# Stores queued behind their data, row tables read 128 columns wide, and the first maxima in another order, in a hybrid Fourier and attention layer

## The chip, the core and the metric

The kernel runs on one core of a Trainium2 chip. The metric is the device time of one execution in microseconds (us), here the median of three runs. The engines have short names in the profile: PE is TensorE (matmuls), PEld its weight loads, DVE is VectorE, ACT is ScalarE, POOL is GpSimd, and SP is SyncE, whose queue issues most of the DMAs. A "q" behind a name (SPq) is that engine's instruction queue.

## The reference

One layer (DEPTH is 1) over 16 meta tokens and 4096 tokens, 4112 rows of 1024 columns. What is computed, cut to its core:

```python
h = concat([meta, x])                                   # 4112 x 1024
u = rmsnorm(h, norm_g)
f_in, f_gate, q, k, v, a_gate = split(u @ w_in)         # 512, 512, 512, 128, 128, 512 columns
fr = real(fftn(f_in as (4112, 8 groups, 64), axes=(rows, 64)))
f_out = (einsum(fr, w_fmix) + b_fmix) * silu(f_gate)
q, k = rope(rmsnorm(q)), rope(rmsnorm(k))               # 8 query heads, 2 key/value heads of 64
a_out = softmax(q k^T / 8) v * silu(a_gate)
h = h + concat([f_out, a_out]) @ w_out
out = rmsnorm(h, final_g)[16:]
```

All tensors are float32. The kernel splits each operand into a float16 high and low part and multiplies three times (high by high, high by low, low by high).

## The kernel before

**Phase A** (`phase_a`, the first 720 us of the profile) goes over 33 row tiles `t` (32 of 128 rows and one of the 16 meta rows). For each tile, `xload` loads the transposed rows, `xsplit` makes the two halves `xh` (ACT, L318) and `xl` (POOL, L319), and `proj` multiplies by the weights: 256 columns of k and v in `tile_kv`, 512 of q in `tile_q`, and twice 512 of gates in `tile_gate`. `xsplit` of the next tile stands ahead of `tile_kv` of the present one, so the halves are made a tile ahead. `tile_kv` also makes the two halves of v (`vst`, ACT L366 and POOL L367, in three buffers `vsb`) and stores them to DRAM (L368, by the helper `store`, L222). `tile_norm` and `tile_stack` finish q and k, and `tile_tr`, which is called a tile later, stores k (by the same helper) and q (on ACT's queue).

Beside the tiles runs the first half of the Fourier group. Each fold `i` (0 to 8) loads 128 columns of rows at four mirrored places (`fold_load`: row scales `rb`, L452, and data `sg`, L454), scales them on POOL (`fold_scale`, L463), adds and subtracts them on DVE (`fold_add`), splits them (`fold_hi`, `fold_lo`) and multiplies them by the Fourier weights of the columns (`fproj`). `fproj` with k = 1 writes results: its inner `put` makes two halves `ahl` (ACT L522, POOL L523, two buffers) and stores them to `acs_d` (L524). Folds 0 to 3 call `put` once and store a part `ge_d` (L532); folds 4 to 7 load that part again (`even_load`, L486) and call `put` three times. The rows of `w_out` are split beside this too (`wo_load`, `wo_split`, stored at L600).

The order of this work is written by hand: `plan` maps slots, four to a tile, to lists of calls, and `deal(slot)` emits them. Fold `i` begins at slot 8 + 23i/2; `w_out` begins at slot `WO0` = 72.

All loads and stores that go through `dma` (`nc.sync.dma_start`) stand in SP's queue in the order in which they are emitted. SP issues them one after another, and waits at a store until its data is there.

**Phase B** (`phase_b`, from 720 us on) is the attention: 32 pairs, one for each of 8 query blocks and 4 head pairs, each with 66 units (`stream`, `step`: two heads by 33 key tiles). A unit multiplies k by q (L1185 to L1194), takes the exponential on ACT (L1199), a rest `rr` on POOL or DVE (L1201), and multiplies by v (L1216 to L1223). For the next pair, 16 groups of row maxima run along (`max_units`: four matmuls L1106, ACT L1111 and DVE L1112 twice each, with four PSUM banks `m`); `red` reduces them to `nm` (DVE L1139), `fin` turns `nm` with a matmul (L1146) and `put` writes the rows into `qB` (ACT L1152, DVE L1153, with a constant `diag`), which the pair's first matmul with `qB` reads (L1190).

Ahead of the first pair stands a prelude: 16 groups and a meta unit for pair 0, and two groups (`AHEAD`) for pair 1, without any attention between.

The second half of the Fourier group (the transform over rows) is a list `flist` that `f_step` takes entries from: "d" is one matmul of a row set with its table (`dft_units`, L895 and L898), "gather" takes the result out of PSUM, "t" is a turn (`trans`, L937 to L944) or the mixing with `w_fmix` and gate (`mix`: matmuls by `mm3`, L86 to L88; early, in the prelude, ACT L990 and POOL L996 and L998; later DVE L992 and POOL L1000), and "gap" lets a unit pass. The first and the last row set (`LAST`) have only 4 rows; their tables `cl` hold 4 columns for each matmul. In the prelude each group is followed by `f_step(11, 2, True)`; then each of the first 264 units calls `f_step(2, 1)` in `block0` until the list is empty. `mix` puts its stores to `mf_d` on a list `held`, which `release` issues (L924) at the next "gather"; its buffers `mos` hold two row sets. When the list is empty, `block0` loads the weights `woh` and `wol` (L1090, L1091), and an assert wants that before unit 258. From pair 4 on, 28 of the pairs carry the output projection of a block (`out_units`, L1296).

Of the kernel before, what the change touches and what calls it, by code (L numbers as in the profile page):

```python
# [32 lines left out]
P = 128  # L33
# [21 lines left out]
def emit(tc, a):  # L55
# [4 lines left out]
    with top:  # L60
# [49 lines left out]
        cl = sh1.tile([P, 2, 2, 18, 4], F16, tag="cl", name="cl")  # L110
# [39 lines left out]
def phase_a(tc, a, pool, mm3, id16, id32, sc):  # L150
# [25 lines left out]
    with ExitStack() as st:  # L176
# [174 lines left out]
        def tile_kv(t):  # L351

            n = xs[t][0]
            rt = rw[:n, pos[t]:pos[t] + 1]
            if t < NT:
                z = live[t] = {k: w2.tile([P, 10, HD], F32, tag=k, name=k) for k in ("sq", "t1", "t2")}
            else:
                z = live[t] = {k: wp.tile([P, 2, HD], F32, name=k + "m") for k in ("sq", "t1", "t2")}
            o = z["o"] = 0 if t < NT else 8
            kvp = proj(t, 0, 256)  # L360
            kp = kvp[:, :P].rearrange("p (h c)->p h c", c=HD)
            S.activation(z["sq"][:n, 8 - o:10 - o], kp, AF.Square, scale=rt)
            vs = w2.tile([P, 2, HD], F32, tag="vs", name="vs")
            S.activation(vs[:n], kvp[:, P:].rearrange("p (h c)->p h c", c=HD), AF.Copy, scale=rt)
            vst = vsb[pos[t] % 3]
            S.activation(vst[:n, :, 0:64], vs[:n], AF.Copy)  # L366
            G.tensor_tensor(out=vst[:n, :, 65:129], in0=vs[:n], in1=vst[:n, :, 0:64], op=ALU.subtract)  # L367
            store(v_d[place[t], :n], vst[:n])  # L368
            rot(t, kp, 8, 10, 1)
# [54 lines left out]
        def tile_tr(t):  # L424
            n, ks = xs.pop(t)[0], kst(t)
            z = live.pop(t)
            store(k_d[place[t] * P:place[t] * P + n], ks[:n].rearrange("p a w b c->p (a w b c)"))
            if t < NT:
                adma(q_d[t * P:(t + 1) * P], z["qs"].rearrange("p h a c->p (h a c)"))
# [53 lines left out]

        def even_load(i):
            fst["ge", i] = w1.tile([P, 512], F32, tag="ge", name="ge")
            dma(fst["ge", i], ge_d[7 - i])  # L486

        def fproj(i, k, x):

# [27 lines left out]
            else:  # L517
                f = fst.pop(("f", i, x))

                def put(g, ty, j):  # L520
                    hl = w2.tile([P, 2, NC_], F16, tag="ahl", name="ahl")[:, :, :nn]
                    S.activation(hl[:, 0], g, AF.Copy)  # L522
                    G.tensor_tensor(out=hl[:, 1], in0=g, in1=hl[:, 0], op=ALU.subtract)  # L523
                    dma(acs_d[ty, :, j, :, cs], hl)  # L524
# [6 lines left out]
                if i < 4:  # L531
                    dma(ge_d[i, :, cs], g)  # L532
                else:

                    ge = fst["ge", i][:, cs]
                    h = w1.tile([P, NC_], F32, tag="fe1", name="fe1")[:, :nn]
                    V.tensor_tensor(out=h, in0=ge, in1=g, op=ALU.add)
                    put(h, 0, 7 - i + 4 * x)
                    V.tensor_tensor(out=g, in0=ge, in1=g, op=ALU.subtract)
                    put(g, 0, 7 - i + 4 * (1 - x))  # L540

        def tail():

# [51 lines left out]
        def wo_split(d):  # L595
            wt, hl = room[:, d % 2], room[:, 2 + d % 2].bitcast(F16).rearrange("p (w c) -> p w c", w=2)
            S.activation(hl[:, 0], wt, AF.Copy, scale=WS)
            V.scalar_tensor_tensor(out=hl[:, 1], in0=wt, scalar=WS, in1=hl[:, 0], op0=ALU.mult, op1=ALU.subtract)
            for w in range(2):
                dma(wo_d[w, :, d], hl[:, w])  # L600


        FOLD0, PER2, SLOTS, WO0 = 8, 23, 4, 72
# [43 lines left out]
        for d in range(10):  # L647
            if d > 1:
                at(WO0 + 3 * d, wo_split, d - 2)
            if d < 8:  # L650
# [133 lines left out]
def phase_b(tc, a, pool, mm3, id32, id16, sc):  # L784
# [10 lines left out]
    with ExitStack() as st:  # L795
# [18 lines left out]
        for t in qB[1]:  # L814
            G.memset(t[0:64], 0.0)
# [3 lines left out]
        V.tensor_copy(diag, id32[0:8, 0:8].unsqueeze(2).broadcast_to([8, 8, P]))  # L819
# [30 lines left out]
        def fix_load():  # L850
            dma(bias, a["bias"])
            V.memset(stk8[0:64], 0.0)
# [19 lines left out]
        def dft_units(i, part, spare):  # L872

            u, odd = seq[i], int(i < 5)
            if part == 0:
                fcur["ct"] = ld["cl"][:, 1 - odd] if u is LAST else ld["cts"].pop(0)
            ct, src = fcur["ct"], ld["acs"][odd]
            mms = []
# [10 lines left out]
            def one(x, slot, chunk, w, first, last):  # L889
# [3 lines left out]
                r = ps[0][0:4 if u is LAST else P, cs]  # L893
                if chunk == 8:
                    T.matmul(r, ct[0:96, x, slot], src[0:96, 8, 0, cs], start=False, stop=last,  # L895
                             skip_group_check=True)
                else:
                    T.matmul(r, ct[:, x, slot + (w == 2)], src[:, chunk, int(w == 1), cs],  # L898
# [23 lines left out]
        def release():  # L922
            while held:
                dma(*held.pop(0))  # L924
# [53 lines left out]
        def mix(u, k, early):  # L978
# [16 lines left out]
            if early:  # L995
                G.tensor_tensor(out=mo[:n], in0=mo[:n], in1=bias[:n].unsqueeze(1).broadcast_to([n, 2, 512]),  # L996
                                op=ALU.add)
                G.tensor_tensor(out=mo[:n], in0=mo[:n], in1=fgu[:n], op=ALU.mult)  # L998
            else:
                G.tensor_tensor(out=mo[:n, ver], in0=mo[:n, ver], in1=fgu[:n, ver], op=ALU.mult)  # L1000
            for ver in vers:
                for p0, w, t0, st in runs_of(u, ver):
                    held.append((rows(mf_d, t0, w, st), mo[p0:p0 + w, ver]))
# [6 lines left out]
        fcur = {}  # L1010

        def f_fill():
            done = []
            for i, u in enumerate(seq):
# [4 lines left out]
                for k, n in enumerate(parts):  # L1019
# [3 lines left out]
                    if i > 4:  # L1023
                        flist.append(("gap", 3))
# [14 lines left out]
        GAPS = (4, 3, 2)  # L1039
        f_fill()  # L1040

        def f_step(n, heavy, early=False):

            while flist:
# [17 lines left out]
                elif k == "gather":  # L1062
# [4 lines left out]
                    release()  # L1067
# [300 lines left out]
        while gs:  # L1368
# [6 lines left out]
            if n == 1:  # L1375
                ld["k_load"](ld["rest"])
            elif n in (7, 10, 13, 16):
# [15 lines left out]
        for k in range(AHEAD):  # L1393
# [4 lines left out]
            if k:  # L1398
                f_step(5, 1, True)
                fin()  # L1400
                put()
                f_step(INIT - 5, 1, True)
# [4 lines left out]
        def block0(g, mid):  # L1407
# [4 lines left out]
            if g < 4 * 66:  # L1412
                f_step(2, 1)
# [185 lines left out]
def shape_constants():  # L1599
# [84 lines left out]
    return {"dch": dch.astype(f), "cd": cd, "cl": cl, "rope": rope, "sgn": sgn}  # L1684
# [54 lines left out]
```

## Time and profile before

| what | value |
|---|---|
| three runs | 3126.31, 3130.44, 3131.52 us; median 3130.44 us |
| the profiled execution | 3128.15 us, its span 3126.4 us, so 1.75 us lie outside the span |
| busy over the span | PE 98%, DVE 72%, ACT 65%, PEld 57%, POOL 55% |
| granted TensorE clock | 0.995 on the mean |
| PE in the chain that ended last | 70% of the span |
| DMA | 235.16 MB, 75 GB/s on the mean |

The profile is of one execution. A row of the timeline has the start in us from the span's start, the time it took in us, the engine, the line, the operation, the tiles as out<-in, the shape and the count, and, in brackets, the idle time of the engine just before it with what ended it. A row of the waits names who waited for whom, with the total in us, the number of times and the longest. A row of the windows has the stretch, its length, then for each engine the busy us and the number of instructions, and at the end the granted TensorE clock, the busy share of the DMA engines and their GB/s. Matmul times are modelled with their latency, so the distance from one start to the next tells what a matmul costs in a dense stream.

### The profile page before, as it was taken

The page shows a single profiled execution, that of the slowest core. Times are in us where ns is not written, and L with a number is a line of the kernel's source. Part 1 is how long each engine was busy: PE and PEld are TensorE (multiplying, and loading weights), DVE is VectorE, ACT ScalarE, POOL GpSimd, SP SyncE. Part 2 cuts the span into 40 slices and gives each one's busy share as a digit, 9 for nine tenths or more (in the row PEclk, how much of TensorE's full clock was granted, in tenths as well). Part 3 has the DMA queues.
Part 4 walks back from the last instruction along what each step waited for, and adds up shares of the span by engine and source line. Part 5 has one row for each costly group of instructions (what it writes and reads, how often), then busy time and mean ns, then how long its engine had stood idle before and what let it go on. Part 6 is the DMA issues. An engine that isn't in the chain of part 4 may idle for free.

```text
span 3126.4 us, 80138 instructions
## 1 busy us (share of the span) xinstructions
PE 3055.6 (98%) x32000; PEld 1792.2 (57%) x32000; DVE 2261.6 (72%) x4866; ACT 2017.9 (65%) x3936; POOL 1732.5 (55%) x1629
## 2 busy tenths in 40 slices
PE   8999999898899999999999999999999999999998
PEld 4555555455566555555555555555555555555564
DVE  7655655565878777777777777777777777777775
ACT  6334233234777677777777777777777777777763
POOL 4665555543666555555555555555555555555553
PEclk9999999999999999999999999999999999999999
DMA  7445444466531221112111211211121112111112
GB/s 254 159 148 180 143 137 141 130 174 201 144 87 32 83 44 37 35 29 49 39 29 29 49 39 29 52 32 29 39 49 29 29 35 52 32 32 29 33 45 71
DMA packets 236763, 235.16 MB, mean 75 GB/s; under 512 B 136948, under 2 KB 180948, under 8 KB 233572
## 3 DMA queue, kind: packets, MB, share of 16 engines
q1 hardware_dynamic: 222564, 204.87, 22.8%
q10 hardware_dynamic: 13824, 25.17, 2.1%
q8 instruction: 250, 4.10, 0.5%
q14 instruction: 125, 1.02, 0.1%
HBM read 131.08 MB, written 66.38 MB: 63 GB/s over the span
## 4 chain that ended last, share of the span: by engine, by line
PE 70%; POOL 4%; DVE 3%; issue 3%; ACT 3%; DMA 2%; SPq 1%; ACTq 0%; POOLq 0%; DVEq 0%
PE o L1216 12%; PE po L1296 9%; PE o L1223 8%; PE s L1189 8%; PE s L1190 7%; PE s L1185 7%; PE m L1106 7%; PE s L1194 5%; PE o L1221 2%; PE o L1219 2%; PE m L1538 1%; ACT pe L1199 1%; POOL rr L1201 1%; PE pd L898 1%; DMA acs_d<-ahl 1%
## 5 line engine op out<-in xcount | busy, mean ns | idle before, releaser
L1199 ACT ACTIVATE pe<-s 128x512 f32<-128x512 f32 x2112 | 1240.1, 610 | 587.9 <-PE s L1194 524.5
L1201 POOL TENSOR_TENSOR rr<-pe 128x512 f16<-128x512 f32 x1014 | 1131.5, 1132 | 824.5 <-ACT pe L1199 819.2
L1201 DVE TENSOR_TENSOR rr<-pe 128x512 f16<-128x512 f32 x1098 | 886.4, 811 | 274.6 <-ACT pe L1199 271.4
L1223 PE MATMUL o<-VV,rr 128*128 128x65 f16 x8448 | 974.8, 193 | 0.3 <-POOL rr L1201 0.3
L1223 PEld LDWEIGHTS <-rr 128*128 128x128 f16 x8448 | 784.5, 98 | 188.1 <-issue 1.4
L1112 DVE CUSTOM_DVE_ANT_0 rl<-m,rl 128x512 f32<-128x512 f32 x1024 | 703.5, 689 | 242.1 <-ACT rl L1111 240.8
L1216 PE MATMUL o<-VV,pe 128*128 128x129 f16 x6336 | 839.5, 221 | 0.8 <-ACT tt L1230 0.8
L1216 PEld LDWEIGHTS <-pe 128*128 128x128 bf16 x6336 | 589.7, 97 | 364.7 <-issue 192.6
L1111 ACT ACTIVATE rl<-m 128x512 f32<-128x512 f32 x1024 | 630.2, 617 | 9.9 <-PE m L1106 5.8
L1190 PE MATMUL s<-qB,K 128*128 128x512 f16 x1088 | 412.0, 379 | 3.5 <-DVE qB L1153 3.5
L1189 PE MATMUL s<-qA,K 128*128 128x512 f16 x1088 | 411.2, 378 | 2.5 <-ACT pe L1199 1.7
L1219 PE MATMUL o<-VV,pe 128*128 128x65 f16 x2112 | 411.3, 195 | 0.0
L1221 PE MATMUL o<-VV,pe 128*128 128x64 f16 x2112 | 410.5, 194 | 0.0
L1185 PE MATMUL s<-qA,K 128*128 128x512 f16 x1024 | 387.5, 378 | 7.9 <-ACT pe L1199 6.5
L330 PE MATMUL ps<-wh,xh 128*128 128x512 f16 (+2 forms) x1032 | 354.2, 355 | 13.1 <-ACT xh L318 12.9
L331 PE MATMUL ps<-wl,xh 128*128 128x512 f16 (+2 forms) x1032 | 354.0, 354 | 2.2 <-DVE wl L301 2.2
L1106 PE MATMUL m<-K,qA 64*128 64x512 f16 x1024 | 305.1, 377 | 9.5 <-ACT rl L1111 6.6
L1106 PE MATMUL m<-K,qB 64*128 64x512 f16 x1024 | 310.9, 377 | 2.1 <-DVE mx L1112 1.6
L333 PE MATMUL ps<-wh,xl 128*128 128x512 f16 x768 | 291.4, 379 | 0.0
L1221 PEld LDWEIGHTS <-pe 128*128 128x128 bf16 x2112 | 209.1, 99 | 0.0
L1219 PEld LDWEIGHTS <-pe 128*128 128x128 bf16 x2112 | 206.5, 98 | 0.0
L1194 PE MATMUL s<-qB,K 64*128 64x512 f16 x512 | 197.9, 387 | 0.0
(219 smaller groups left out, 4368.9 us busy)
## 6 DMA issues: line engine op xcount, KB each, us to landing
room<-x SPq DMA_DIRECT2D x32, 512.0 KB
xt<-xt SPq DMA_DIRECT2D x32, 512.0 KB
sg<-fx SPq DMA_DIRECT2D x16, 1024.0 KB
xr<-x SPq DMA_DIRECT2D x32, 512.0 KB
out<-yo SPq DMA_DIRECT2D x32, 512.0 KB
fg_d<-g ACTq DMA_DIRECT2D x32, 256.0 KB
ag_d<-g ACTq DMA_DIRECT2D x32, 256.0 KB
q_d<-qs ACTq DMA_DIRECT2D x32, 256.0 KB
```

The lines of the kernel that those rows point to most:

```text
L1106: T.matmul(ts[x], q[e][p][:, e, s * P:(s + 1) * P], K[kv][64 * e:64 * e + 64, 0, c0:c0 + 512], start=True, stop=True)
L1111: S.activation(rl, ts[e], AF.Relu)
L1112: V.tensor_tensor_reduce(out=rl, in0=ts[2 + e], in1=rl, scale=1.0, scalar=-3.0e38, op0=ALU.add, op1=ALU.max, accum_out=mx[:, s, e, o:o + 1])
L1185: T.matmul(s, K[kv][:, 0, cs], qa, start=False, stop=False, skip_group_check=True)
L1189: T.matmul(s, K[kv][:, 0, cs], qa, start=True, stop=False)
L1190: T.matmul(s, K[kv][:, 1, cs], qb, start=False, stop=True)
L1199: S.activation(pe, d["s"], AF.Exp, scale=HD ** -0.5)
L1201: eng.tensor_tensor(out=rr, in0=pe, in1=hi, op=ALU.subtract)
L1216: T.matmul(o[:, c0:c0 + 129], hi[:, cs], va, start=t == 0 and s == 0, stop=t == NT, skip_group_check=True)
L1219: T.matmul(o[:, c0:c0 + 65], hi[:, cs], vh, start=False, stop=t == NT, skip_group_check=True)
L1221: T.matmul(o[:, c0:c0 + 64], hi[:, cs], vl, start=False, stop=t == NT, skip_group_check=True)
L1223: T.matmul(o[:, c0:c0 + 65], rr[:, cs], vh, start=False, stop=t == NT, skip_group_check=True)
```

## The change

- Phase A: the store of v moves from `tile_kv` to `tile_tr`, a tile later. `put` and the store of `ge_d` go onto a list `lag`, which is emptied at the next `put`, `fproj`, `even_load` or `tail`. The stores of the split `w_out` come three slots after the split, and `WO0` is 70.
- Tables: `cl` is stored flat with 124 columns of zeros behind it, and a matmul of a `LAST` set reads 128 columns from its place on, so that it writes 128 rows of which 4 are used.
- Held stores: `release` is called in each `f_step` and issues what is at least 2 steps old in the prelude and 6 steps old later, no longer at "gather".
- The early `mix` makes its two POOL operations for each half of 512 columns by itself.
- The list: gaps of 2 in place of 3 behind a "gather", 3 in place of 4 ahead of a turn; in `block0` one and two matmuls in turn in place of two.
- Order: the clearing of `qB[1]` (POOL), the making of `diag` (DVE) leave the start of phase B and stand after 9 and after 4 groups; `stk8` is cleared on POOL in place of DVE; for pair 1's second group `fin` and `put` of pair 0 come ahead of the Fourier matmuls, not after five of them.

```diff
-        cl = sh1.tile([P, 2, 2, 18, 4], F16, tag="cl", name="cl")
+        cl = sh1.tile([P, 2, 36 * 4 + 124], F16, tag="cl", name="cl")
...
-            store(v_d[place[t], :n], vst[:n])
             rot(t, kp, 8, 10, 1)
...
             z = live.pop(t)
+            store(v_d[place[t], :n], vsb[pos[t] % 3][:n])
             store(k_d[place[t] * P:place[t] * P + n], ks[:n].rearrange("p a w b c->p (a w b c)"))
...
+        lag = []
+
+        def lag_out():
+            while lag:
+                dma(*lag.pop(0))
+
         def even_load(i):
+            lag_out()
...
                 def put(g, ty, j):
+                    lag_out()
...
-                    dma(acs_d[ty, :, j, :, cs], hl)
+                    lag.append((acs_d[ty, :, j, :, cs], hl))
...
-                    dma(ge_d[i, :, cs], g)
+                    lag.append((ge_d[i, :, cs], g))
...
+        def wo_store(d):
+            hl = room[:, 2 + d % 2].bitcast(F16).rearrange("p (w c) -> p w c", w=2)
             for w in range(2):
                 dma(wo_d[w, :, d], hl[:, w])
...
-        FOLD0, PER2, SLOTS, WO0 = 8, 23, 4, 72
+        FOLD0, PER2, SLOTS, WO0 = 8, 23, 4, 70
...
                 at(WO0 + 3 * d, wo_split, d - 2)
+                at(WO0 + 3 * d + 3, wo_store, d - 2)
...
-        for t in qB[1]:
-            G.memset(t[0:64], 0.0)
...
-        V.tensor_copy(diag, id32[0:8, 0:8].unsqueeze(2).broadcast_to([8, 8, P]))
...
-            V.memset(stk8[0:64], 0.0)
+            G.memset(stk8[0:64], 0.0)
...
+            def table(rows, x, slot):
+                if u is LAST:
+                    o = 4 * (18 * x + slot)
+                    return ld["cl"][rows, 1 - odd, o:o + P]
+                return ct[rows, x, slot]
...
-                r = ps[0][0:4 if u is LAST else P, cs]
+                r = ps[0][:, cs]
...
-        def release():
-            while held:
-                dma(*held.pop(0))
+        def release(age=0):
+            while held and held[0][0] + age <= fcur["tick"]:
+                dma(*held.pop(0)[1:])
...
-            if early:
-                G.tensor_tensor(out=mo[:n], in0=mo[:n], in1=bias[:n].unsqueeze(1).broadcast_to([n, 2, 512]),
-                                op=ALU.add)
-                G.tensor_tensor(out=mo[:n], in0=mo[:n], in1=fgu[:n], op=ALU.mult)
-            else:
+            for ver in vers:
+                if early:
+                    G.tensor_tensor(out=mo[:n, ver], in0=mo[:n, ver], in1=bias[:n], op=ALU.add)
                 G.tensor_tensor(out=mo[:n, ver], in0=mo[:n, ver], in1=fgu[:n, ver], op=ALU.mult)
...
-                        flist.append(("gap", 3))
+                        flist.append(("gap", 2))
...
-        GAPS = (4, 3, 2)
+        GAPS = (3, 3, 2)
...
         def f_step(n, heavy, early=False):
-
+            fcur["tick"] += 1
+            release(2 if early else 6)
...
-                    release()
...
+            elif n == 4:
+                V.tensor_copy(diag, id32[0:8, 0:8].unsqueeze(2).broadcast_to([8, 8, P]))
+            elif n == 9:
+                for t in qB[1]:
+                    G.memset(t[0:64], 0.0)
...
             if k:
-                f_step(5, 1, True)
                 fin()
                 put()
-                f_step(INIT - 5, 1, True)
+                f_step(INIT, 2, True)
...
-                f_step(2, 1)
+                f_step(2 if g % 2 else 1, 1)
```

More of the change, by code (lines that the diff above doesn't have):

```diff
@@ L520, in put @@
                 def put(g, ty, j):
+                    lag_out()
                     hl = w2.tile([P, 2, NC_], F16, tag="ahl", name="ahl")[:, :, :nn]
@@ L542, in tail @@
         def tail():
+            lag_out()
             pd = []
@@ L875, in dft_units @@
             if part == 0:
-                fcur["ct"] = ld["cl"][:, 1 - odd] if u is LAST else ld["cts"].pop(0)
+                fcur["ct"] = None if u is LAST else ld["cts"].pop(0)
             ct, src = fcur["ct"], ld["acs"][odd]
+            def table(rows, x, slot):
[3 more added lines that the diff above has]
+                return ct[rows, x, slot]
             mms = []
@@ L892, in one @@
                 cs = slice(0, NC_) if x == 0 else slice(NC_, 512)
-                r = ps[0][0:4 if u is LAST else P, cs]
+                r = ps[0][:, cs]
                 if chunk == 8:
-                    T.matmul(r, ct[0:96, x, slot], src[0:96, 8, 0, cs], start=False, stop=last,
+                    T.matmul(r, table(slice(0, 96), x, slot), src[0:96, 8, 0, cs], start=False, stop=last,
                              skip_group_check=True)
                 else:
-                    T.matmul(r, ct[:, x, slot + (w == 2)], src[:, chunk, int(w == 1), cs],
+                    T.matmul(r, table(slice(0, P), x, slot + (w == 2)), src[:, chunk, int(w == 1), cs],
                              start=first, stop=False, skip_group_check=True)
@@ L1002, in mix @@
                 for p0, w, t0, st in runs_of(u, ver):
-                    held.append((rows(mf_d, t0, w, st), mo[p0:p0 + w, ver]))
+                    held.append((fcur["tick"], rows(mf_d, t0, w, st), mo[p0:p0 + w, ver]))
             if k != 0 and u + 2 < len(sets):
@@ L1009, in phase_b @@
         flist = []
-        fcur = {}
+        fcur = {"tick": 0}
         def f_fill():
@@ L1683, in shape_constants @@
     sgn[97:128, 0] = -1
-    return {"dch": dch.astype(f), "cd": cd, "cl": cl, "rope": rope, "sgn": sgn}
+    return {"dch": dch.astype(f), "cd": cd, "cl": np.concatenate([cl.reshape(P, 2, 144), np.zeros((P, 2, 124), f16)], axis=2), "rope": rope, "sgn": sgn}
 def layout(x, meta_tokens, norm_g, w_in, w_fmix, b_fmix, q_norm_g, k_norm_g, w_out, final_g):
```

## The prediction

> **What bounds the kernel now.** I read the windows first, then the waits by engine, then the timeline at the stalls. The windows by stage:
>
> ```profile
> 500.00:650.00 150.00, 137.24 (x788) 78.50 (x787) 78.42 (x167) 47.16 (x84) 75.72 (x62) 0.97 0.48 146
> 720.00:800.00 80.00, 61.54 (x515) 37.44 (x513) 50.82 (x117) 43.01 (x80) 36.88 (x24) 0.89 0.59 177
> 800.00:1100.00 300.00, 284.26 (x3619) 176.60 (x3617) 237.99 (x467) 216.20 (x423) 193.14 (x179) 1.00 0.28 80
> 1150.00:3000.00 1850.00, 1848.78 (x22163) 1087.30 (x22162) 1434.36 (x3131) 1389.08 (x2750) 1035.04 (x1046) 1.00 0.14 37
> ```
>
> The second number is PE's busy time. From 1150 to 3000 PE idles 1.2 us: that stretch is bound by matmuls, and no edit touches it. Idle time stands in three places: 12.8 us in the last folds of phase A (500 to 650), 18.5 us in the prelude (720 to 800), 15.7 us beside the Fourier list (800 to 1100). In the first two the granted clock is low as well: 3% of 150 us is 4.5 us, 11% of 80 us is 8.8 us, partly while PE idles anyway. So some 60 us at most are within reach of this change.
>
> Who waits in the last folds, from the waits of PE, SP and POOL between 470 and 650:
>
> ```profile
> PE ps L330 <- ACT xh L318: 5.2, 3, 2.9
> PE ps L335 <- POOL xl L319: 4.2, 3, 3.2
> PE pf L88 <- POOL fl L482: 3.3, 1, 3.3
> SPq L222 <- POOL vst L367: 44.1, 7, 13.6
> SPq L600 <- DVE room L598: 24.6, 5, 17.4
> POOL sg L463 <- DMA sg<-fx: 22.4, 2, 12.6
> POOL ahl L523 <- ACT ahl L522: 22.5, 13, 5.0
> ```
>
> PE waits for halves that POOL and ACT make, 12.7 us in all. POOL itself stood idle for 22.4 us in two waits for fold data. And SP, which loads that data, stood at stores whose data wasn't there. The timeline shows one case whole, SP's and POOL's rows:
>
> ```profile
> 552.73 0.42 POOL L367 TENSOR_TENSOR vst<-vs,vst 128x128 f16<-128x128 f32 x1
> 553.17 0.33 SPq L222 DMA_DIRECT2D v_d<-vst  x1
> 557.37 0.47 SPq L454 DMA_DIRECT2D sg<-fx  x1
> 565.74 4.65 POOL L463 TENSOR_TENSOR sg<-sg,rb 128x1024 f32<-128x1024 f32 x2 [12.60 <-DMA sg<-fx]
> ```
>
> POOL finishes `vst`, only then SP gets past the store, issues the row scales and `sg`, and POOL, whose next work needs `sg`, waits 12.60 us. The load was issued when its consumer was already there.
>
> **The change, part A: stores in phase A.** The store of v goes behind a tile's q, norm and gates in SP's queue, so it passes the loads dealt in the first two slots (`sg`, `rb`, `w_out` rows) and stands beside the store of k, whose data is as old. `wo_store` goes three slots back, the last `put` of an `fproj` to the next `fproj`. The DMAs are the same in number and size. The early limit on `sg` is then its buffer, free since the DVE step at slot b+5 of a fold, and `rb`, free after POOL's at b+7; the load stands at b+11. A slot is a quarter tile, about 5 us (33 tiles in 720 us), so the load gets some 15 us of lead, against a wait of 12.60. Nothing new waits: `vst` has three buffers, and a store a tile late is still a tile ahead of their reuse. What stays: with two `ahl` buffers and three `put`s, the third waits for the first store, on ACT, and those 22.5 us of POOL behind ACT remain. So A takes back between 3 us (the `ahl` chain simply is next) and 17 us (12.8 idle and 4.5 of clock). I take 13, nearer the top: the two `sg` waits alone are longer than all of PE's.
>
> **Part B: the prelude.** At its start:
>
> ```profile
> 725.16 1.98 DVE L819 CAST diag<-id 8x1024 f16<-8x1024 f32 x1 [4.56 <-DMA k_d<-ks]
> 727.76 0.64 ACT L909 ACTIVATE bs<-pd 4x264 f32<-4x264 f32 x2 [7.32 <-DVE bs L852]
> 729.07 0.58 PE L1106 MATMUL m<-K,qA 64*128 64x512 f16 x1 [6.63 <-ACT rl L1111]
> 725.18 0.29 POOL L812 MEMSET K<- 128x224 f16 x1 [5.76 <-DMA k_d<-ks]
> 725.65 4.16 POOL L815 MEMSET qB<- 64x1024 f16 x4
> 730.06 0.52 POOL L973 MEMSET fgu<- 32x512 f32 x1
> ```
>
> PE waits for ACT, ACT for the clearing of `stk8` behind `diag` on DVE, and all for the last store of k, which stays. On POOL `stk8` comes behind 0.5 us (725.18 to 725.65), two small clearings, 0.52 for `fgu`, and takes about 0.52 (half the rows of `fgu` more, same columns): done near 727.1, and ACT starts 0.6 sooner than at 727.76. The 4.16 us of `qB` move behind group 9; there POOL waits for ACT's next `mo` anyway:
>
> ```profile
> 760.49 2.35 POOL L996 TENSOR_TENSOR mo<-mo,bs 128x1024 f32<-128x1024 f32 x1 [3.09 <-ACT mo L990]
> ```
>
> so 3.09 of the 4.16 are covered and 1.1 delay a mixing that PE doesn't wait for: nothing, and 1.1 if that cover is gone. SP, which stood at `fgu`'s clearing, gets on 4.1 us earlier. `diag`'s 1.98 us now lie between groups on DVE: 0 to 2, I take 0.5.
>
> Later in the prelude some small DVE operations take far too long, each while a POOL operation of 1024 columns runs:
>
> ```profile
> 748.59 2.35 POOL L998 TENSOR_TENSOR mo<-mo,fgu 128x1024 f32<-128x1024 f32 x1
> 748.79 2.31 DVE L944 COPY thl<-thl 128x512 f16<-128x512 f16 x1
> 757.58 0.29 DVE L944 COPY thl<-thl 128x512 f16<-128x512 f16 x1
> 789.30 2.35 POOL L996 TENSOR_TENSOR mo<-mo,bs 128x1024 f32<-128x1024 f32 x1 [4.14 <-ACT mo L990]
> 789.40 2.79 DVE L1153 TENSOR_TENSOR qB<-row,diag 8x1024 f16<-8x1024 f16 x1 [1.58 <-ACT row L1152]
> 792.24 0.58 PE L1190 MATMUL s<-qB,K 128*128 128x512 f16 x1 [2.64 <-DVE qB L1153]
> ```
>
> The copy took 0.29 us free and 2.31 beside POOL, ending when POOL does. Halves of about 1.2 us let it in 1.1 us sooner, which PE gets. `put` with its ACT row and this `qB` passes, on ACT and POOL, the last early mixing: it runs before that POOL operation begins, and PE has ten more matmuls ahead of L1190. So the 2.64 us go; next late is ACT's `mo` and its table. Of the clock's 8.8 us I count 1.
>
> Against it: a held store now goes two steps later and behind one of the `VV` loads. The mixing two sets on needs its buffer:
>
> ```profile
> 768.68 1.23 ACT L990 ACTIVATE mo<-t 128x512 f32<-128x512 f32 x2 [3.78 <-DMA mf_d<-mo]
> VV<-v_d SPq DMA_DIRECT2D x4, 516.0 KB
> ```
>
> SP stood at `mix`'s own `fgu` load until POOL was done, so the store hardly moves in time, but 516 KB go ahead of it: at the window's 177 GB/s 2.9 us, and POOL is done about 1 us earlier. I charge 1.5. B: 0.6 - 0.5 + 1.1 + 2.6 + 1 - 1.5 = 3.3, with ends of -9 (2.9 at each of four mixings, `diag` in full, no clock) and 13 (all of the clock, neither charge).
>
> **Part C: beside the attention.** Two table matmuls in a unit, with 4 columns (first three rows) and with 128:
>
> ```profile
> 1042.27 0.38 PE L1190 MATMUL s<-qB,K 128*128 128x512 f16 x1
> 1042.58 0.37 PE L898 MATMUL pd<-acs,cl 128*4 128x248 f16 x2
> 1042.88 0.23 PE L1216 MATMUL o<-VV,pe 128*128 128x129 f16 x1
> 878.74 0.38 PE L1190 MATMUL s<-qB,K 128*128 128x512 f16 x1
> 878.95 0.38 PE L898 MATMUL pd<-acs,ct 128*128 128x248 f16 x2
> 879.17 0.22 PE L1216 MATMUL o<-VV,pe 128*128 128x129 f16 x1
> L898 PEld LDWEIGHTS <-cl x96: 80/83/87, 714.8 to 1057.9; 128*4 128x4 f16 x96
> L898 PEld LDWEIGHTS <-ct x288: 95/98/152, 721.0 to 991.8; 128*128 128x128 f16 x144
> ```
>
> From L1190 to L1216 it is 0.61 us with 4 columns and 0.43 with 128: entering and leaving the narrow shape costs 0.18. 52 matmuls, two a unit, are 26 units: 4.7 us, of which I take 4, between 0 and 4.7, as PE is the late engine there. A load by itself is longer with 128 columns, 98 ns against 83, but in the 0.43 us it is hidden.
>
> The Trainium skill ("TensorE: Matmul & The Clock Gate", section "LDWEIGHTS (loading the stationary operand)") speaks against the wider tables: there a load takes its number of columns over 1.2, in ns, so 3 ns for 4 columns and 107 for 128. By it, exposed loads would make C's tables an estimated 5.4 us dearer (52 x 104 ns) in place of 4 cheaper, and the sum below 13.9 in place of 23.3. The trace's 83 ns for 4 columns doesn't agree.
>
> The list: 8 parts of 14 matmuls and one of 52 at two a unit are 82 units; 11 sets at 12 units and 9 gaps of 3, and 2, make 243. After: sets at 11, gaps of 2, and 1.5 matmuls a unit: 121 + 18 + 2 + 115 = 256, so 8 units before pair 4, within the assert's 258. PE's extra work in a unit with two matmuls falls by a quarter; the gathers on DVE (busy 238 of 300) come closer together. Of the 15.7 us idle I take 3 back, between -5 (a third more of it) and 9 (over half of it gone). C: 7. The list's end moves 13 units of 1.14 us (300 us / 264), 15 us:
>
> ```profile
> 1075.14 3.23 SPq L924 DMA_DIRECT2D mf_d<-mo  x5
> 1105.92 0.69 ACT L1254 ACTIVATE hl<-mf 128x512 f16<-128x512 f32 x1
> ```
>
> The last store then goes near 1090, 16 us before its first reader: covered; without that cover pair 4 begins late by what is missing.
>
> **Sum.** 13 + 3.3 + 7 = 23.3. The profiled execution took 3128.15 us (span 3126.4 and 1.75 around it): 3104.9 after. It lies 2.3 below the median of 3130.44, so the median comes to 3107.
>
> **Rivals.** First, in A the `ahl` chain on ACT takes the stall over: A gives 3, the sum is 13, 3117. For it: 22.5 us of POOL behind ACT; against: those waits are short, 13 of them. Second, slower: in the prelude ACT blocks at `mo` for the held store of two sets before, and group maxima queue behind it. Nineteen steps in the 60 us from 729 to 789 are 3.2 us each; two steps and 2.9 us of `VV` are 9.3 a mixing, at four mixings 37 us, minus the 23.3: 3144. It decides from 6 us a mixing; for it the 3.78 us wait that is there, against it SP's own wait, which held the store back already. Third, the queue isn't the cause: SP merely waits at other stores, loads come as late as before, the rest of B and C cancel: 3130. Against it stands the row at 553.17. Fourth, exposed wide weight loads: 52 x 98 ns is 5.1 us lost in place of 4 gained, 3116; against it the 0.43 us.
>
> **Chances.** Forecast 0.62, first rival 0.17, second 0.08, third 0.09, fourth 0.04. The range goes from all terms at their best (17 + 13 + 13.7, 3087) up to A at 3 with nothing else, 3127. A measurement tells about 0.2% (6.3 us) from no change: faster 0.83 (forecast, first, fourth), same 0.09, slower 0.08.
>
> **What would show it.** Right: SP's waits at L222 and L600 nearly gone between 470 and 650, no wait of POOL for `sg`, PE above 145 of 150 us there, no wait at the first L1190, the 128-column `cl` at 0.43 us. Wrong: PE's idle time unchanged in 500 to 650, or ACT's wait for `mf_d` above 6 us each time in the prelude.

## The result, and the profile after

The changed kernel took 3093.39 us on the median of four runs (3092.27 to 3098.02); the kernel before took 3129.82 on the same chip. The ratio is 0.9888, with a 95% interval of 0.9871 to 0.9905: 36 us by the medians, where 23.3 were forecast. The time lies inside the range (3087 to 3127) and below the forecast of 3107. Two executions, both of the kernel before with part B, ran at a granted clock of 0.44 and 0.65 and took 7745 and 4339 us; they are in no figure below. The profiled execution took 3098.02 us (span 3096.2), the slowest of the four, and is 30.2 us of span shorter than the profiled execution of before.

The windows by stage, of the changed kernel:

```profile
500.00:650.00 150.00, 150.00 (x897) 87.51 (x896) 89.78 (x196) 53.56 (x96) 84.82 (x67) 1.00 0.52 154
700.00:710.00 10.00, 5.23 (x39) 3.66 (x37) 4.30 (x16) 1.52 (x3) 2.88 (x3) 0.89 0.28 102
710.00:722.00 12.00, 7.66 (x34) 3.50 (x33) 3.94 (x12) 4.60 (x9) 1.75 (x6) 0.53 0.61 154
800.00:1100.00 300.00, 287.84 (x3713) 184.11 (x3710) 238.60 (x481) 222.14 (x438) 197.12 (x185) 1.00 0.26 70
```

In the last folds PE is busy for 150.00 of 150 us at the full clock (before: 137.24 at 0.97). Beside the Fourier list it idles 12.2 us (before 15.7). Between the two PE still loses time: from 700 to 722 it is busy for 12.9 of 22 us, and the granted clock falls to 0.53.

The waits of SP and POOL between 470 and 650, of the changed kernel:

```profile
SPq L601 <- DVE room L606: 60.4, 6, 11.6
SPq L488 <- POOL ahl L531: 48.8, 13, 14.3
...
POOL t L389 <- DVE rq L387: 25.2, 8, 7.1
POOL ahl L531 <- ACT ahl L530: 24.6, 14, 5.1
```

SP's wait at the store of v (44.1 us) and POOL's for `sg` (22.4 us) are gone. SP's waiting as a whole isn't: it stands 60.4 us at the load of the next `w_out` rows (L601) and 48.8 at the `ahl` stores, each more than before (24.6 and 16.8 at the stores of `w_out`, 39.1 at those of `ahl`), and PE loses nothing by it. What counts is which load stands behind the wait, not how long the queue stands.

What happens between 683 and 715, in the timeline of the changed kernel (rows of SP, ACT, POOL and PE):

```profile
683.59 0.43 SPq L98 DMA_DIRECT2D acs<-acs_d  x1
685.06 0.67 ACT L395 ACTIVATE g<-ps,rw 128x512 f32<-128x512 f32 x1
695.27 0.33 ACTq L396 DMA_DIRECT2D ag_d<-g  x1
695.65 1.06 ACT L594 ACTIVATE wvh<-wv 128x1024 f16<-128x1024 f32 x1 [9.91 <-DMA acs<-acs_d]
696.87 2.86 PE L913 MATMUL pd<-acs,cl 128*128 128x264 f16 x24
706.01 0.67 ACT L395 ACTIVATE g<-ps,rw 128x512 f32<-128x512 f32 x1
706.73 0.37 PE L1119 MATMUL m<-K,qA 64*128 64x512 f16 x1 [4.24 <-ACT g L395]
711.21 0.29 POOL L824 MEMSET K<- 128x224 f16 x1 [5.55 <-DMA k_d<-ks]
712.45 0.52 POOL L861 MEMSET bs<- 64x512 f32 x1
714.30 0.58 PE L1119 MATMUL m<-K,qA 64*128 64x512 f16 x1 [4.84 <-ACT rl L1124]
```

ACT makes a gate at 685.06 and stands at its store until 695.27, though the data was there at 685.73. Only then comes the chain of the last tile, and PE waits 4.24 us for its last piece, `g`. The last store of k is late with it, so `K`, the clearing of `stk8` (`bs`, 712.45), the gather behind it and with it `rl` are late too: 4.84 us more. This second wait isn't new (the kernel before waits 6.63 us for `rl`, at 729.07); the first is. From the first Fourier matmul (696.87) to the first maximum (706.73) it is 9.9 us, where it was 5.7 before.

### The profile page after: what moved, and what is told of

Its sections match the earlier page's. It is cut to its first block, busy times and chain, and to the rows that moved or that the text cites. A ratio compares the mean times of both kernels' runs of the same rounds, so it can differ in the third digit from the quotient of the medians.

```text
span 3096.2 us, 80211 instructions
## 1 busy us (share of the span) xinstructions
PE 3040.8 (98%) x32000; PEld 1795.2 (58%) x32000; DVE 2268.7 (73%) x4865; ACT 2016.2 (65%) x3936; POOL 1732.6 (56%) x1642
## 4 chain that ended last, share of the span: by engine, by line
PE 90%; POOL 2%; DVE 2%; issue 2%; ACT 2%; DMA 1%; SPq 0%; ACTq 0%; POOLq 0%; DVEq 0%
PE o L1229 12%; PE po L1309 10%; PE o L1236 8%; PE s L1202 8%; PE s L1198 7%; PE s L1203 7%; PE m L1119 7%; PE ps L331 6%; PE ps L330 6%; PE s L1207 5%; PE ps L333 5%; PE o L1234 2%; PE o L1232 2%; PE m L1555 1%; PE pf L86 1%
```

## The experiments

Twelve kernels were run. The first table has the times, each with its ratio to runs of the kernel before on the same chip.

| kernel | median us | ratio [95% interval] |
|---|---|---|
| changed | 3093.39 | 0.9888 [0.9871, 0.9905] |
| changed, again | 3096.63 | 0.9891 [0.9874, 0.9907] |
| before + part A | 3111.36 | 0.9931 [0.9918, 0.9943] |
| before + v store only | 3113.57 | 0.9938 [0.9925, 0.9950] |
| before + wide tables | 3127.11 | 0.9983 [0.9974, 0.9992] |
| before + spread list | 3123.58 | 0.9970 [0.9958, 0.9981] |
| before + part B | 3125.02 | 0.9977 [0.9968, 0.9986] |
| changed, release at the gather | 3093.43 | 0.9879 [0.9866, 0.9892] |
| changed, early mixing undivided | 3099.81 | 0.9901 [0.9888, 0.9914] |
| changed, put late again | 3095.76 | 0.9889 [0.9877, 0.9902] |
| changed, gates' last stores late | 3090.11 | 0.9871 [0.9856, 0.9886] |
| changed, Fourier load early | 3099.84 | 0.9902 [0.9887, 0.9916] |
| the last stores late, release at the gather | 3088.96 | 0.9867 [0.9842, 0.9892] |

The second has the stages of the profiled executions, worked out from the starts of three instructions in each trace: the first Fourier matmul, the first exponential and the 265th (at the end of the fourth pair). After that one, all of them need 2026.4 to 2027.2 us.

| kernel | to the first Fourier matmul | from there to the first exponential | to the 265th |
|---|---|---|---|
| before | 714.8 | 78.1 | 306.4 |
| changed; again | 696.9; 696.3 | 76.9; 76.6 | 295.6; 295.6 |
| before + part A | 696.5 | 77.7 | 306.6 |
| before + v store only | 696.7 | 81.3 | 306.9 |
| before + wide tables | 716.6 | 78.1 | 303.0 |
| before + spread list | 721.2 | 78.0 | 300.8 |
| before + part B | 716.9 | 73.6 | 307.4 |
| changed, release at the gather | 695.6 | 75.9 | 294.1 |
| changed, early mixing undivided | 696.7 | 79.6 | 295.0 |
| changed, put late again | 695.7 | 77.5 | 294.7 |
| changed, gates' last stores late | 697.0 | 64.7 | 295.6 |
| changed, Fourier load early | 696.5 | 82.1 | 294.9 |
| the last stores late, release at the gather | 695.7 | 68.9 | 295.5 |

**Part A alone.** The kernel before with the three moves of stores in phase A:

```diff
-            store(v_d[place[t], :n], vst[:n])          # tile_kv
+            store(v_d[place[t], :n], vsb[pos[t] % 3][:n])   # tile_tr
...
-                    dma(acs_d[ty, :, j, :, cs], hl)
+                    lag.append((acs_d[ty, :, j, :, cs], hl))
...
+                at(WO0 + 3 * d + 3, wo_store, d - 2)
```

> The kernel before with all of part A and nothing else (the v store behind q, norm and gates; the folds' stores one step later; w_out's split stores three slots later). Theory one, the queue is the cause: PE busy 150 of 150 us from 500 to 650 as in the changed kernel, the last projection matmul near 696.7 instead of 714.5 (17.8 us earlier), of which about 4 are lost again at the first group of the attention, since ACT's chain of the last tile now runs into the loads of the Fourier step: in all 14 us faster, 3116. Rival, the ahl chain on ACT takes the stall over: 3 us, 3127, and the rest of the 17.8 came from part B and the clock. Second rival, the give-back belongs to part B's new order and not to A: 18 us, 3112.

The first Fourier matmul came at 696.5 as in the changed kernel, and PE was busy for 150.00 of 150 us from 500 to 650. By the ratio it is 21.6 us, more than the 14 and 18 of the two theories that make the queue the cause. The `ahl` chain didn't take the stall over. From the first Fourier matmul to the first maximum it took 7.6 us, between the 5.7 of before and the 9.9 of the changed kernel: part of the give-back stands here already, without part B.

**The store of v alone.** Only the first two lines of the diff above.

> The kernel before with only the store of v moved behind the tile's q, norm and gates. Theory one, this store alone held the loads of sg (44.1 us of SP at it, 22.4 of POOL for sg): most of A, 10 to 13 us, 3117 to 3120, POOL's wait for sg gone. Rival, SP merely stands at the next unready store, those of ahl or of w_out's halves (24.6 us of SP): under 5 us, 3125 or more, POOL's wait for sg still above 10 us.

The waits of SP and POOL from 470 to 650, of the kernel before with the v store moved, and its window:

```profile
SPq L524 <- POOL ahl L523: 58.2, 17, 9.8
SPq L600 <- ACT room L597: 32.4, 7, 15.3
SPq L600 <- DVE room L598: 24.2, 7, 13.0
...
POOL sg L463 <- DMA sg<-fx: 7.7, 1, 7.7
```

```profile
500.00:650.00 150.00, 149.37 (x894) 87.08 (x893) 89.30 (x197) 50.67 (x92) 80.66 (x65) 1.00 0.53 155
```

One store moved gives 19.4 of the 21.6 us by the ratios, and the intervals overlap. SP stands longer than before at the stores of `ahl` and `w_out`, as the rival said; but only one wait for `sg` is left, of 7.7 us, and PE is busy for 149.37 us. The list `lag` and the later `wo_store` have no part in it that these runs can tell: the 3.6 us by which the prelude is longer here than with all of part A are of one profile each.

**The tables alone.**

```diff
-        cl = sh1.tile([P, 2, 2, 18, 4], F16, tag="cl", name="cl")
+        cl = sh1.tile([P, 2, 36 * 4 + 124], F16, tag="cl", name="cl")
...
-                r = ps[0][0:4 if u is LAST else P, cs]
+                r = ps[0][:, cs]
...
+                    return ld["cl"][rows, 1 - odd, o:o + P]
```

> The kernel before with only the tables of the small rests read 128 columns wide. Theory one, entering and leaving the 4-column shape costs 0.18 us in each of 26 units: 4.7 us, 3125.7, from L1190 to L1216 0.43 us with cl as with ct. Rival, a 128-column load costs more than a 4-column one where it is exposed: up to 5 us slower, 3135. Second rival, PE is not late there and idles more instead: no change, 3130.

From the first to the 265th exponential it is 303.0 us in place of 306.4, 3.4 less, or 0.13 us in each of 26 units; the ratio says 5.3 us, with an interval of 2.5 to 8.1. The timeline of this kernel, a unit with two table matmuls:

```profile
1042.80 0.38 PE L1196 MATMUL s<-qB,K 128*128 128x512 f16 x1
1043.02 0.37 PE L904 MATMUL pd<-acs,cl 128*128 128x248 f16 x2
1043.23 0.22 PE L1222 MATMUL o<-VV,pe 128*128 128x129 f16 x1
```

From the score matmul to the one by v it is 0.43 us, as with `ct`, where the 4-column table needed 0.61. The wide load isn't exposed.

**The spread list alone.**

```diff
-                        flist.append(("gap", 3))
+                        flist.append(("gap", 2))
...
-        GAPS = (4, 3, 2)
+        GAPS = (3, 3, 2)
...
-                f_step(2, 1)
+                f_step(2 if g % 2 else 1, 1)
```

> The kernel before with only the Fourier list spread (one or two matmuls a unit in turn, gaps 2, 3, 3, 2). The stretch with the list became 10.9 us shorter in the changed kernel, against 7 predicted. Theory one, the 4.7 of the tables are in it and the spreading gives the rest, 6 us: 3124, with PE idle below 11 of 300 us from 800 to 1100. Rival, the spreading gives the 3 us predicted and the other 3 came from elsewhere (held stores, part B's order): 3127. Second rival, the spreading does nothing alone: 3130.

The window beside the list, of this kernel:

```profile
800.00:1100.00 300.00, 287.93 (x3647) 178.14 (x3646) 238.31 (x474) 219.18 (x430) 197.26 (x182) 1.00 0.29 83
```

From the first to the 265th exponential it is 300.8 us, 5.6 less, and PE's idle time from 800 to 1100 falls from 15.7 to 12.1 us, not below 11. The ratio says 9.4 us (6.0 to 13.2), more than the stage shows: the executions of a kernel without part A differ by some us in phase A, and this stage is what the edit touches.

**Part B alone.** All moves of the prelude, on the kernel before:

```diff
-            V.memset(stk8[0:64], 0.0)
+            G.memset(stk8[0:64], 0.0)
...
+            elif n == 9:
+                for t in qB[1]:
+                    G.memset(t[0:64], 0.0)
...
+            for ver in vers:
+                if early:
+                    G.tensor_tensor(out=mo[:n, ver], in0=mo[:n, ver], in1=bias[:n], op=ALU.add)
...
-                f_step(5, 1, True)
                 fin()
                 put()
-                f_step(INIT - 5, 1, True)
+                f_step(INIT, 2, True)
```

> The kernel before with only the changes of the prelude: stk8 on POOL, diag behind the fourth group and qB's clearing behind the ninth, early mixing steps in halves, put ahead of the last Fourier units, held stores released by age. Measured alone, A gave 0.9931, the tables 0.9983 and the spread list 0.9970, together 36 us, all that the whole change gave. Theory one, B is nothing in sum, since its gains are met by a dearer store: 3129 to 3133, the first exponential as late behind the first Fourier matmul as in the kernel before (78.1 us), ACT still waiting for mf_d. Rival, the 3.3 us predicted: 3129, 74.8 us. Second rival, B only works where A has made room: slower alone, 3134 or more.

The prelude is 4.4 us shorter (73.6 in place of 78.1), and the ratio says 7.2 us (4.4 to 10.0). Neither theory one nor the slower rival holds: B alone gives more than the 3.3 predicted. But the four parts add up, by their ratios, to 21.6 + 7.2 + 5.3 + 9.4 = 43.5 us, and the whole gives 35; the five intervals, each some 3 to 5 us to either side, leave room for much of that difference. In the stages it is smaller. On top of part A, B's stage gains 0.8 us (77.7 to 76.9) in place of 4.4. So A and B together lose 3.6 us there of what each gives alone.

**Three parts of B undone.** The held stores let go at the gather again (first), the early mixing in steps of 1024 columns again (second), and `fin` and `put` back between the Fourier steps (third), each in the changed kernel:

```diff
-            release(2 if early else 6)      # f_step
+                    release()               # at "gather"
```

> The changed kernel with the held stores let go at the gather again, as in the kernel before. ACT waits twice for mf_d in the prelude of the changed kernel, 5.2 us, and not at all where part A stands alone. Theory one, the release by age costs what was charged, 1.5 us, up to these 5.2: 3088 to 3092 without it. Rival, the held store costs nothing, since the Fourier list or the maxima are late anyway: 3093.4. Second rival, the later release was needed, so that a store not yet ready does not hold the loads of the gates: slower without it, 3098.

```diff
-                    G.tensor_tensor(out=mo[:n, ver], in0=mo[:n, ver], in1=bias[:n], op=ALU.add)
+                G.tensor_tensor(out=mo[:n], in0=mo[:n], in1=bias[:n].unsqueeze(1).broadcast_to([n, 2, 512]),
+                                op=ALU.add)
```

> The changed kernel with the early mixing steps of 1024 columns on POOL again instead of halves. Theory one, as predicted: a small copy on DVE takes 2.3 us beside the long POOL step and 0.3 free, and PE gets 1.1 us: 3094.5, with thl copies of 2 us again. Rival, halves make no difference, since DVE then waits for the second half or PE has other matmuls: 3093.4. Second rival, halves delay the mixing, two more instructions and the second step of a half behind another: faster without them, 3091.

```diff
+                f_step(5, 1, True)
                 fin()
                 put()
-                f_step(INIT, 2, True)
+                f_step(INIT - 5, 1, True)
```

> The changed kernel with fin and put back between five and six units of the last Fourier steps ahead of the first scores. Theory one, as predicted: the 2.64 us of PE's wait for qB come back: 3096. Rival, where A stands alone that wait is already 1.7 us, so half of it comes back: 3095. Second rival, the first exponentials are bound elsewhere: 3093.4.

With the release at the gather the median is 3093.43, which the runs don't tell apart from the changed kernel's 3093.39 and 3096.63; the intervals of the three ratios overlap. ACT's waits for `mf_d` in the prelude, one row each from the changed kernel, the changed kernel again, and the release at the gather:

```profile
ACT mo L1005 <- DMA mf_d<-mo: 5.2, 2, 3.1
```

```profile
ACT mo L1005 <- DMA mf_d<-mo: 2.2, 1, 2.2
```

```profile
ACT mo L1005 <- DMA mf_d<-mo: 1.9, 1, 1.9
```

The 5.2 us belonged to one execution; the same kernel had one wait of 2.2 in the next. That fits neither theory of the repeat as a whole: one of the two waits is gone, but one of more than 1 us is left, and the span is 3095.2 us, not near 3091.

The undivided mixing makes the prelude 2.6 to 3.0 us longer (79.6), and the median 3 to 6 us higher (3098.63 to 3100.14, where the changed kernel's eight runs lie between 3092.27 and 3098.12). The rows of that kernel, with DVE's copy beside POOL and a later small step of DVE, and the same two steps in the changed kernel:

```profile
733.82 2.35 POOL L1013 TENSOR_TENSOR mo<-mo,fgu 128x1024 f32<-128x1024 f32 x1
734.03 2.30 DVE L959 COPY thl<-thl 128x512 f16<-128x512 f16 x1
767.28 2.09 DVE L1154 SCALAR_TENSOR_TENSOR nm<-mm,met 128x8 f16<-128x8 f32 x1
```

```profile
734.89 0.69 DVE L959 COPY thl<-thl 128x512 f16<-128x512 f16 x1
767.42 0.94 DVE L1152 SCALAR_TENSOR_TENSOR nm<-mm,met 128x8 f16<-128x8 f32 x1
```

So the halves give more than the 1.1 us predicted. PE waits 0.95 us behind that copy, which is the predicted gain; the rest is mostly the step that writes `nm`, behind which PE waits 2.50 us for its next maxima, in place of 0.94. `put` gave less than predicted: its median of 3095.76 lies between the two of the changed kernel, and with it back the prelude is 77.5, 0.5 to 0.9 us longer, and PE's wait for `qB` is 0.9 us in that kernel, not 2.64:

```profile
PE s L1203 <- DVE qB L1166: 0.9, 1, 0.9
```

**The changed kernel again, and its last stores.** To see how much one profile says, the changed kernel ran a second time, beside two edits of the end of phase A. In the one the four stores of the last two tiles' gates go to the end of ACT's work in phase A:

```diff
+            if pos[t] < NT - 1:
                 adma(dst[t * P:(t + 1) * P], go)
+            else:
+                gst.append((dst[t * P:(t + 1) * P], go))
...
+        for z in gst:
+            adma(*z)
         tile_tr(order[-1])
```

In the other the 2 MB load for the Fourier step goes ahead:

```diff
-        at(b + 12, ld["acs_load"], 1)
-        at(b + 10, lambda: ld["q_start"]())
-        at(b + 10, fix_load)
+        at(b + 10, ld["acs_load"], 1)
+        at(b + 12, lambda: ld["q_start"]())
+        at(b + 12, fix_load)
```

> The changed kernel, unchanged, once more, beside the two edits below on the same chip. Its profiled run took 3098.0 where its other three took 3092.3 to 3093.9, and the kernel with the held stores let go at the gather took 3094.2 with its profile, the whole difference lying between the first Fourier matmul and the 66th exponential. Theory one, ACT's two waits for mf_d (5.2 us) are what the release by age costs: they stand in this profile too. Rival, they belong to that one run: this profile has none of more than 1 us and a span near 3091, and the release by age costs nothing.

> The changed kernel with the four stores of the last two tiles' gates put at the end of ACT's work in phase A. In the changed kernel ACT stands at such a store from 685.75 to 695.27, until a load of 2 MB for the Fourier step has landed, and the last tile's chain comes 4 us later after its last matmul than in the kernel before, so PE waits 4.2 us for g at the first group. Theory one, this wait is the give-back: without it the first group comes 6 us behind the last projection as before, not 10, and the time falls by 4: 3089. Rival, the stores of q on the same queue wait in its place, or the last k store and the keys' load are late anyway: the wait moves to the exponentials' first table, 3093.

> The changed kernel with the 2 MB load for the Fourier step put two slots earlier and the loads of q and of the mixing weights two later. Theory one, ACT's store then waits for an earlier landing and the last tile's chain is 4 us sooner: 3089. Rival, whatever load stands there holds ACT's store, now that of q and the weights: the first group no earlier, or the first Fourier matmul later: 3093 to 3097.

With the late stores the median is 3090.11, beside 3096.63 of the changed kernel again, and none of the four runs of the one (3085.72 to 3093.37) reaches those of the other (3093.74 to 3098.12); the first four runs of the changed kernel, on another chip, go down to 3092.27, and the intervals of the ratios overlap. ACT and PE in the timeline, and the windows, of the kernel with the late stores:

```profile
681.49 0.67 ACT L397 ACTIVATE g<-ps,rw 128x512 f32<-128x512 f32 x1
687.35 1.06 ACT L599 ACTIVATE wvh<-wv 128x1024 f16<-128x1024 f32 x1 [5.20 <-DVE wv L597]
702.57 0.39 PE L1126 MATMUL m<-K,qA 64*128 64x512 f16 x1
```

```profile
700.00:710.00 10.00, 9.01 (x72) 5.81 (x72) 3.48 (x11) 4.41 (x9) 1.78 (x6) 1.00 0.82 225
710.00:722.00 12.00, 12.00 (x107) 7.68 (x106) 9.18 (x28) 8.03 (x16) 1.80 (x2) 1.00 0.42 134
```

ACT goes on at 687.35 in place of 695.65. The first maximum comes 5.6 us behind the first Fourier matmul, neither wait of PE is there, and the clock stays at 1.00. So the late stores take away more than the give-back: the wait for `rl`, which the kernel before had too, goes with it. The prelude is 64.7 us in this profile, 12.3 less than in the changed kernel. This execution was the fastest of its four, so 12.3 is more than the kernel gains on the whole; the medians say 3.3 to 6.5.

With the load early it got worse. The waits of ACT and PE between 670 and 715, of that kernel:

```profile
ACT qs L410 <- DMA fg_d<-g: 17.2, 1, 17.2
...
PE m L1119 <- ACT g L395: 8.1, 1, 8.1
```

The rival was right in its mechanism, and its 3093 to 3097 was still too low for the measured 3099.84: ACT now stands 17.2 us around an earlier store, and PE waits 8.1.

What such a store waits for stands in the traces' semaphore records. All 814 transfers of a trace report their landing on eight semaphores, 101 or 102 transfers to each, and ahead of a transfer the issuing queue often waits for the semaphore that the transfer itself is going to use. In the changed kernel the store at 695.27 uses the semaphore of the load `acs` that SP issued at 683.59; that load has wholly landed at 695.20, and ACT's wait for its semaphore is over at 695.22. With the load early, the store that stands (issued at 688.53) shares its semaphore with a load of q that SP issued at 682.25 and that has landed at 688.46. So a store is held by one particular earlier transfer, with whose data it has nothing to do. The kernel before has such a store as well, at 703.03, behind a load of `qB` that has landed at 702.96; there its data was ready 7.8 us earlier, but a tile's matmuls were still left for PE.

**Both together.** The late stores, and the release at the gather.

> Both edits that may help, on the changed kernel: the gates' stores of the last two tiles at the end of ACT's work, and the held stores let go at the gather again. Theory one, the release by age costs 2 to 4 us, which the kernel with it undone showed in its profile (first Fourier matmul to 66th exponential 147.4 us in place of 149.4 to 149.7), though not in its median: 3087, PE's wait of 2.5 us for thl gone. Rival, its cost is nothing and the difference was that of single runs: 3090 as with the late stores alone. Second rival, the late stores have made the queue so full that the early release now blocks the loads of the gates: 3093.

The median of 3088.96 isn't told apart from 3090.11. It lies between the 3087 of theory one and the rival's 3090, but PE's wait of 2.5 us for `thl`, which theory one had gone, is still there, so nothing here speaks for a cost of the release. The row of the wait that is left in this kernel's profile, and its windows:

```profile
707.72 0.58 PE L1126 MATMUL m<-K,qA 64*128 64x512 f16 x1 [4.56 <-ACT rl L1131]
```

```profile
700.00:710.00 10.00, 5.34 (x34) 2.71 (x32) 2.13 (x7) 2.92 (x6) 1.81 (x6) 0.79 0.59 184
710.00:722.00 12.00, 12.00 (x83) 6.59 (x82) 8.37 (x25) 6.43 (x12) 0.00 (x0) 0.89 0.70 183
```

Here the clearing on POOL came 2.7 us later than with the late stores alone (705.87 against 703.22), PE waited 4.56 us for what follows it, and the clock fell, for a shorter time than in the changed kernel. The prelude is 68.9 us. So the second of the two waits is there in one of these two profiles and not in the other; the first is in neither. This version and the one before it are the fastest that were run.

## Why the prediction was right, and where its sizes were wrong

**Part A: the mechanism was right, the size too small.** The term was 13 us, between 3 and 17; it measured 17.9 to the first Fourier matmul in the two profiles of before and after, and 21.6 by the ratio of A alone. Two things were mis-sized. The 13 discounted an idle time (12.8 us) and a lost clock (4.5 us) which both went in full, as the window shows. And the 4.5 came from one execution. From 500 to 650, of the kernels with the spread list alone and with part B alone, where phase A is as before:

```profile
500.00:650.00 150.00, 134.55 (x754) 75.34 (x753) 78.79 (x159) 48.61 (x88) 75.67 (x56) 0.95 0.47 141
```

```profile
500.00:650.00 150.00, 137.74 (x775) 78.06 (x774) 78.84 (x167) 47.80 (x86) 77.72 (x62) 0.94 0.48 143
```

The clock was 0.94 and 0.95 there, not 0.97, and the first Fourier matmul came at 716.6 to 721.2 in three such executions, not at 714.8. The profile of before was the luckiest of four in this stage, so a bound taken from it alone was too low. With part A, alone or with the rest, all nine profiles lie between 695.6 and 697.0. The reason given for A stands: with the v store alone moved, 7.7 of POOL's 22.4 us for `sg` are left, and PE's idle time falls from 12.8 to 0.6 us.

**"Nothing new waits" was the step that failed.** It looked at buffers. With phase A 18 us earlier, ACT's last stores meet the loads for the Fourier step, and PE waits 4.24 us at the first maximum. Part A alone shows it with 1.9 us more from the first Fourier matmul to the first maximum, the v store alone with 3.6 (9.3 us), and moving the gates' last stores takes it away. The store waited for a semaphore that it shares with a load on SP's queue, so its own data and buffers, which the prediction went by, couldn't show this wait. Which transfers share one changed when the 2 MB load was moved; by what rule they are assigned isn't shown.

**Part B: 3.3 predicted, 4.4 alone, 0.8 on top of A.** By its terms:
- `stk8` on POOL: 0.6 predicted. PE's longest wait for `rl` fell from 6.6 to 6.0 us with B alone, in the row below. Right, as long as the last store of k doesn't come late.
- `qB`'s clearing: predicted free, since a mixing that PE doesn't wait for covers it. The cover was the wrong one. In the timeline of the changed kernel:

```profile
742.05 3.62 POOL L1394 MEMSET qB<- 64x1024 f16 x4
742.55 3.27 DVE L959 COPY thl<-thl 128x512 f16<-128x512 f16 x1
745.87 0.23 PE L88 MATMUL t<-wvh,thl 128*128 128x128 f16 x1 [1.80 <-DVE thl L959]
```

It stands beside DVE's copy, which takes 3.27 us in place of 0.3, and PE waits 1.80 us for that. The prediction had the very row that should have warned of it, the 2.31 us copy, and used it for the mixing alone. The Trainium skill ("SBUF — State Buffer", section "🔬 SBUF: two separate sides") says that DVE, in operations of some kinds, and GpSimd share one pair of ports, which whoever starts first holds for its whole instruction while the other is blocked. The trace agrees that DVE is blocked, and is harsher: the copy didn't get in between the four clearings either, and ended 0.15 us after the last.
- Halves: 1.1 predicted, 2.6 to 3.0 in the prelude. The term counted one copy, and that copy gave 0.95; it left out the step that writes `nm`, which gave 1.6 more.
- `put`: 2.6 predicted, 0.5 to 0.9. With the rest of the prelude changed, the wait for `qB` that it removes was 0.9 us.
- The held stores: a charge of 1.5, and none measurable. ACT's waits for `mf_d` were 5.2 and 2.2 in two executions of the same kernel, against 4.8 before.
- `diag` (0.5) and the clock (1) weren't tried by themselves.

The row of B alone for the first point:

```profile
PE m L1101 <- ACT rl L1106: 6.6, 3, 6.0
```

**Part C: 7 predicted, 10.8 measured** (306.4 to 295.6). The shape change was 4 and measured 3.4; the spreading was 3 and measured 5.6, the mis-sized term, in a range from -5 to 9. The other 1.8 show only where both are in, and aren't explained. The reason for the tables stands: 0.43 us with 128 columns. By the price of a load in the Trainium skill ("TensorE: Matmul & The Clock Gate", section "LDWEIGHTS (loading the stationary operand)"), which the prediction weighed, they would have cost an estimated 5.4 us; they gave 3.4.

**The rivals.** That the `ahl` chain takes over fell with part A alone: POOL's wait for ACT there stayed (24.6 us, before 22.5), and PE didn't feel it. That held stores block ACT fell at its own point of decision: no wait for `mf_d` was above 3.1 us, where it needed 6. That the queue isn't the cause fell with the one store moved. Exposed loads fell with the tables alone.

**The sum.** In the two profiles it is 17.9 + 1.2 + 10.8 = 29.9 of the 30.2 us of span, against 13 + 3.3 + 7 = 23.3. Two terms that were too careful outweighed the give-back that wasn't foreseen.

## What to carry to other kernels

Ask of each instruction that issues transfers what stands behind it: here one store put behind its data was worth some 20 us, and longer waits of the same queue at other stores were worth nothing. A store whose data is ready can still stand, here for a load that shares its semaphore; the trace tells which. When a stage gets shorter, look at the next boundary, where its last stores and the next stage's first loads now meet, before the gain is booked. And take the bound of a clock loss, or of any wait on a transfer, from several executions: one profile of the kernel before was the best of four.

## What the runs showed of the hardware

A long wait of PE can cost more than itself. Behind two waits of 4.24 and 4.84 us the granted clock was 0.53 from 710 to 722; behind one of 4.56 us it was 0.79 and 0.89 in the two windows; in the kernel with the late stores, where no wait of PE in the prelude is above 1.9 us, it stayed at 1.00 (64.7 us, in place of 68.9 and 76.9). But the clock also fell without one long wait: in the changed kernel it was at half again from 752.1 to 755.5, and the longest gap of PE in the 30 us before is 1.80 us. The Trainium skill ("TensorE: Matmul & The Clock Gate", section "🔬 Part 1: The HAM clock gate (the "warmup" mystery)") states that the array drops to half its clock after an idle window of about 3.4 us and needs about as much sustained work to come back. The three long waits agree with the first, the drop at 752.1 doesn't. Coming back took longer here: the clock was full again 7.1 us after the second of the two waits was over (714.30 to 721.39), and 4.8 us after the single one (707.72 to 712.56).

A store on ACT's queue, its data ready, stood for 9.5 us until a load of SP's queue that uses the same semaphore had landed.

A DVE copy beside four GpSimd clearings in a row waited for all four (3.27 us). Reading 128 columns of a table, 124 of them unused, was 0.13 us a unit cheaper than reading 4.
